# A two-layer diffusion trunk on one core: modulation matmuls of the first stage in 16 blocks, all token transposes ahead of it, small constants loaded later

## The chip, the core and the metric

The kernel runs on one core of a Trainium2 chip. The metric is the device time of one execution in microseconds. Below, PE is TensorE, DVE is VectorE, ACT is ScalarE, POOL is GpSimd and SP is SyncE, which here does nothing but issue DMAs.

## The reference

Two layers work on 256 latent tokens and 256 context tokens of width 2048, all in float32. The change lies in how layer 0 begins:

```python
shift, scale, gate = jnp.split(jax.nn.silu(c) @ w_ada[li] + b_ada[li], 3, axis=-1)
shift_c, scale_c, gate_c = jnp.split(jax.nn.silu(c_ctx) @ w_ada[li] + b_ada[li], 3, axis=-1)
h = rms_norm(x, g_pre[li]) * (1.0 + scale[:, None]) + shift[:, None]
hc = rms_norm(xc, g_pre[li]) * (1.0 + scale_c) + shift_c
p = h @ w_in[li]
pc = hc @ (w_in[li] if need_ctx else w_in[li][:, :N_KV_COLS])
```

After that each layer has four token mixers (windowed attention, latent attention, a recurrence, pooling), a gated merge and an output projection.

## The kernel before

**Products.** Every large product is taken in two halves: a weight tile `raw` is split by `wunit` into `whi` (ACT, L443) and `wlo` (DVE, L445, with L447 for the odd 64 columns), the activations are kept as `hh` and `hl`, and `prod` adds three matmuls of 128x128 by 512 tokens (L458 `whi`·`hh`, L459 `whi`·`hl`, L461 `wlo`·`hh`).

**The first stage.** `chunks_by_k` goes over the 16 blocks of 128 channels two at a time (`k0` = 0, 2, ... 14). For each `k0` it does three groups of four output tiles, positions 0 to 11; eleven tiles have six matmuls, the one at position 7 is 64 wide and has four, so that a step of `k0` has 70 matmuls. Each tile's sum goes to SBUF: by ACT for `k0` = 0 (L496), by a DVE add afterwards (L498). After each tile the generator `pre` is advanced by one piece; it prepares `hh` and `hl` of the next two channel blocks.

**What `pre` does.** `start(k0)` needs scale and shift of 256 channels. `ada_chunk` takes them from the 2048-row product of SiLU(c) and SiLU(c_ctx) with `w_ada`: for scale and for shift four loads of 512 KB (`adaw`, ring of six buffers), each followed by sixteen weight-loads-and-multiplies on 32-column strips (L251; the trace counts eight matmul records to a load). ACT copies the result (`adaS`, L256), PE turns it (`adaT`, L260), DVE reduces it to `aT` and `bT`. Then `prenorm_out` transposes the normalised tokens of these channels on PE (L394, `n000p` and so on), and ACT and DVE make `hh` (L399), a scaled copy (L400) and `hl` (L401) from the PSUM tile. Each of these is a piece of its own behind one output tile: eight visits to `ada` with one load each, two `adaT` pairs, two groups of four transposes per step.

**Order around it.** Tile schedules the instructions; `issued_after(last_main[0])` ties a piece of `pre` to the last matmul ahead of it, `urgent()` raises its priority. SP issues DMAs in order, so a load that waits for its buffer holds those behind it. The small constants (`late_constants`, POOL's queue) are issued once the last token piece is normalised (`after`, L119).

## Time and profile before

| | |
|---|---|
| median of three runs | 2889.99 us (2888.51 to 2897.6) |
| the profiled execution's own time | 2890.45 us |
| its span in the profile | 2888.7 us |
| PE busy | 2817.6 us, 98% of the span |
| DVE / ACT / POOL busy | 1682.4 / 1083.9 / 99.2 us |
| loads and stores | 457.65 MB, mean 158 GB/s |

The span is the profiled execution from its first to its last instruction; 1.75 us of its own time lie around it. In the line of forty slices PE has a 5 in the first slice of 72 us and 9 in nearly all others, while the DMA line begins with 8, 7 and 6, its highest digits.

### The profile page before, as it was taken

The page shows a single profiled execution, that of the slowest core. Times are in us where ns is not written, and L with a number is a line of the kernel's source. Part 1 is how long each engine was busy: PE and PEld are TensorE (multiplying, and loading weights), DVE is VectorE, ACT ScalarE, POOL GpSimd, SP SyncE. Part 2 cuts the span into 40 slices and gives each one's busy share as a digit, 9 for nine tenths or more (in the row PEclk, how much of TensorE's full clock was granted, in tenths as well). Part 3 has the DMA queues.
Part 4 walks back from the last instruction along what each step waited for, and adds up shares of the span by engine and source line. Part 5 has one row for each costly group of instructions (what it writes and reads, how often), then busy time and mean ns, then how long its engine had stood idle before and what let it go on. Part 6 is the DMA issues. An engine that isn't in the chain of part 4 may idle for free.

```text
span 2888.7 us, 40002 instructions
## 1 busy us (share of the span) xinstructions
PE 2817.6 (98%) x15693; PEld 2368.6 (82%) x15693; DVE 1682.4 (58%) x2686; ACT 1083.9 (38%) x1656; POOL 99.2 (3%) x188
## 2 busy tenths in 40 slices
PE   5999999999999999999999999999999999999998
PEld 2567877887787877788888887888789999999997
DVE  2667757777456655565443566667546545554465
ACT  3225644333223222222222345556433444444443
POOL 1000010000000000000000011000200000000000
PEclk9999999999999999999999999999999999999999
DMA  8762215435444544454555457533333666666664
GB/s 275 253 197 81 81 57 168 121 121 161 156 149 138 177 143 153 146 166 156 153 160 159 155 185 244 188 112 87 96 95 114 185 183 190 183 190 184 194 215 166
DMA packets 307276, 457.65 MB, mean 158 GB/s; under 512 B 19976, under 2 KB 131040, under 8 KB 307088
## 3 DMA queue, kind: packets, MB, share of 16 engines
q1 hardware_dynamic: 294848, 429.98, 48.4%
q0 software_dynamic: 7136, 18.64, 2.1%
q10 hardware_dynamic: 5104, 6.48, 0.6%
q8 instruction: 123, 2.02, 0.3%
q14 instruction: 65, 0.53, 0.1%
HBM read 443.40 MB, written 11.62 MB: 158 GB/s over the span
## 4 chain that ended last, share of the span: by engine, by line
PE 82%; issue 6%; DVE 6%; DMA 4%; ACT 1%; POOL 1%; SPq 0%; DVEq 0%; POOLq 0%; ACTq 0%
DMA adv_1w<-in_w_ada_dram 2%; PE L0stps L459 1%; PE ada L251 1%; DVE wlo L445 1%; PE L0stps L458 1%; PE L0stps L461 1%; PE o10p L1138 1%; PE o10p L1139 1%; PE o10p L1137 1%; PE o01p L1138 1%; PE o01p L1139 1%; PE o01p L1137 1%; DMA adv_0w<-in_w_ada_dram 1%; DMA adaw<-in_w_ada_dram 1%; DVE adv_0a L290 1%
## 5 line engine op out<-in xcount | busy, mean ns | idle before, releaser
L443 ACT ACTIVATE whi<-raw 128x1024 fp32r<-128x1024 f32 (+2 forms) x608 | 638.9, 1051 | 1383.5 <-issue 57.7
L445 DVE TENSOR_TENSOR wlo<-raw,whi 128x1024 fp32r<-128x1024 f32 (+1 forms) x608 | 734.2, 1209 | 572.0 <-ACT whi L443 555.3
L290 DVE SCALAR_TENSOR_TENSOR adv_3a<-adv_3w,csil,adv_3a 128x512 f32<-128x512 f32 x105 | 73.8, 747 | 85.9 <-DMA adv_3w<-in_w_ada_dram 85.7
L290 DVE SCALAR_TENSOR_TENSOR adv_1a<-adv_1w,csil,adv_1a 128x512 f32<-128x512 f32 x105 | 74.5, 747 | 78.0 <-DMA adv_1w<-in_w_ada_dram 77.9
L290 DVE SCALAR_TENSOR_TENSOR adv_0a<-adv_0w,csil,adv_0a 128x512 f32<-128x512 f32 x105 | 73.5, 747 | 66.1 <-DMA adv_0w<-in_w_ada_dram 65.8
L290 DVE SCALAR_TENSOR_TENSOR adv_2a<-adv_2w,csil,adv_2a 128x512 f32<-128x512 f32 x105 | 73.8, 747 | 42.9 <-DMA adv_2w<-in_w_ada_dram 42.5
L459 PE MATMUL L0stps<-hl,whi 128*128 128x512 f32 x192 | 79.9, 416 | 3.8 <-DVE hl L401 3.3
L458 PE MATMUL L0stps<-hh,whi 128*128 128x512 f32 x192 | 79.0, 426 | 2.1 <-ACT hh L399 1.0
L461 PE MATMUL L0stps<-hh,wlo 128*128 128x512 f32 x176 | 69.8, 396 | 0.0
L251 PE MATMUL ada<-adaw,csil 128*32 128x256 f32 x512 | 44.2, 425 | 17.6 <-DMA adaw<-in_w_ada_dram 17.6
L458 PEld LDWEIGHTS L0stps<-hh,whi 128*128 128x128 f32 x192 | 36.1, 188 | 25.4 <-issue 14.8
L459 PEld LDWEIGHTS L0stps<-hl,whi 128*128 128x128 f32 x192 | 36.4, 189 | 19.7 <-issue 8.6
L1138 PE MATMUL o01p<-wlo,hh 128*128 128x512 f32 x128 | 50.2, 393 | 2.1 <-DVE wlo L445 2.1
L1138 PE MATMUL o10p<-wlo,hh 128*128 128x512 f32 x128 | 49.9, 390 | 0.5 <-DVE wlo L445 0.5
L1139 PE MATMUL o01p<-whi,hl 128*128 128x512 f32 x128 | 49.9, 390 | 0.0
L1137 PE MATMUL o00p<-whi,hh 128*128 128x512 f32 x128 | 49.9, 390 | 0.0
L1139 PE MATMUL o00p<-whi,hl 128*128 128x512 f32 x128 | 49.9, 390 | 0.0
L1138 PE MATMUL o00p<-wlo,hh 128*128 128x512 f32 x128 | 49.8, 389 | 0.0
L1137 PE MATMUL o10p<-whi,hh 128*128 128x512 f32 x128 | 49.7, 390 | 0.1
L1139 PE MATMUL o10p<-whi,hl 128*128 128x512 f32 x128 | 49.8, 389 | 0.0
L1137 PE MATMUL o01p<-whi,hh 128*128 128x512 f32 x128 | 49.6, 390 | 0.0
L251 PEld LDWEIGHTS ada<-adaw,csil 128*32 128x32 f32 x512 | 11.1, 114 | 43.0 <-issue 27.2
(2355 smaller groups left out, 8434.5 us busy)
## 6 DMA issues: line engine op xcount, KB each, us to landing
raw<-in_w_in_dram SPq DMA_DIRECT2D x352, 512.0 KB, 3.7
raw<-in_w_out_dram SPq DMA_DIRECT2D x96, 512.0 KB, 4.4
adaw<-in_w_ada_dram SPq DMA_DIRECT2D x64, 512.0 KB, 5.3
raw<-in_w_in_dram SPq DMA_DIRECT2D x256, 128.0 KB, 2.4
raw<-in_w_branch_dram SPq DMA_DIRECT2D x64, 512.0 KB, 3.7
adv_0w<-in_w_ada_dram SPq DMA_DIRECT2D x32, 512.0 KB, 3.7
adv_1w<-in_w_ada_dram SPq DMA_DIRECT2D x32, 512.0 KB, 4.2
adv_2w<-in_w_ada_dram SPq DMA_DIRECT2D x32, 512.0 KB, 4.3
```

The source lines that it names most:

```text
L251: last_ada[0] = mm(out=ps[32 * q:32 * q + 32, :256], lhsT=csil32[:, 4 * u + q, :], rhs=raw[:, q, :], start=(u == 0), stop=(u == 3))
L290: stt(out=acc[r], in0=raw[:, kk, :], scalar=sc, in1=acc[r], op0=ALU.mult, op1=ALU.add)
L443: act(out=hi[:, :, :width], in_=raw[:, :, :width], func=AF.Copy)
L445: tt(out=lo[:, :, :w], in0=raw[:, :, :w], in1=hi[:, :, :w].bitcast(F32), op=ALU.subtract)
L458: mm(out=out, lhsT=w, rhs=xh, start=first, stop=False)
L459: last_main[0] = mm(out=out, lhsT=w, rhs=xl, start=False, stop=last and wd == 64)
L461: last_main[0] = mm(out=out, lhsT=lo[:, kk, o:o + 128], rhs=xh, start=False, stop=last)
L1137: mm(out=pss[t], lhsT=a, rhs=hi[:, kk, :], start=(k == 0), stop=False)
L1138: mm(out=pss[t], lhsT=a, rhs=lo[:, kk, :], start=False, stop=False)
L1139: mm(out=pss[t], lhsT=b, rhs=hi[:, kk, :], start=False, stop=(k == KT - 1))
```

## The change

Each modulation product (256 columns of scale or of shift) is issued as one block of its four loads, behind the tiles at positions 0 and 5 of a step; the turn of both, in one PSUM tile with four transposes, stands behind position 7. The transposes of all 16 channel blocks stand ahead of the stage, copied from PSUM to SBUF tiles `n0t` by ACT and DVE in turns; `hh` and `hl` are made from these. For `j` = 0 alone the block is urgent. `late_constants` is called when `hl` of `k0` = 4 has been written.

```diff
--- before.py
+++ after.py
@@ -239,7 +239,7 @@
     def issued_after(ins):
         return tc.issue_after(ins.ins if hasattr(ins, "ins") else ins)
 
-    def ada_chunk(l, part, j, ring):
+    def ada_units(l, part, j, ring):
 
         c0 = part * D + 256 * j
         ps = paux(f"ada{l}_{part}_{j}")
@@ -249,26 +249,28 @@
                 nc.sync.dma_start(out=raw, in_=I["w_ada"][l, 512 * u:512 * u + 512, c0:c0 + 256].rearrange("(k p) n -> p k n", p=128))
             for q in range(4):
                 last_ada[0] = mm(out=ps[32 * q:32 * q + 32, :256], lhsT=csil32[:, 4 * u + q, :], rhs=raw[:, q, :], start=(u == 0), stop=(u == 3))
-            if u < 3:
-                yield
         S_ = slot(f"adaS{l}_{part}_{j}")
-        S = S_[:, :256]
-        act(out=S, in_=ps[:, :256], func=AF.Copy)
-        pt = paux(f"adaT{l}_{part}_{j}")
         with urgent():
+            act(out=S_[:, :256], in_=ps[:, :256], func=AF.Copy)
+        return S_
+
+    def ada_turn(l, j, S1, S0):
+
+        pt = paux(f"adaT{l}_{j}")
+        for i, S_ in enumerate((S1, S0)):
             for q in range(2):
-                nc.tensor.transpose(pt[:, 128 * q:128 * q + 128], S[:, 128 * q:128 * q + 128], ident)
-        free(S_)
-        red = small(f"adar{l}_{part}_{j}").rearrange("p (a b) -> p a b", b=2)
-        nc.vector.tensor_reduce(out=red, in_=pt[:, :256].rearrange("p (c g r) -> p c r g", c=2, g=4)[:, :, 0:2, :], axis=AX.X, op=ALU.add)
-        bias = BT[:, 48 * l + 16 * part + 2 * j:48 * l + 16 * part + 2 * j + 2].unsqueeze(2).to_broadcast([128, 2, 2])
-        if part == 0:
-            tt(out=bT[l][:, 2 * j:2 * j + 2, :], in0=red, in1=bias, op=ALU.add)
-        elif part == 1:
-            tt(out=red, in0=red, in1=bias, op=ALU.add)
-            g = VT[:, 16 * l + 2 * j:16 * l + 2 * j + 2].unsqueeze(2).to_broadcast([128, 2, 2])
-            stt(out=aT[l][:, 2 * j:2 * j + 2, :], in0=red, scalar=1.0, in1=g, op0=ALU.add, op1=ALU.mult)
-        yield
+                nc.tensor.transpose(pt[:, 256 * i + 128 * q:256 * i + 128 * q + 128], S_[:, 128 * q:128 * q + 128], ident)
+            free(S_)
+        for i, part in enumerate((1, 0)):
+            red = small(f"adar{l}_{part}_{j}").rearrange("p (a b) -> p a b", b=2)
+            nc.vector.tensor_reduce(out=red, in_=pt[:, 256 * i:256 * i + 256].rearrange("p (c g r) -> p c r g", c=2, g=4)[:, :, 0:2, :], axis=AX.X, op=ALU.add)
+            bias = BT[:, 48 * l + 16 * part + 2 * j:48 * l + 16 * part + 2 * j + 2].unsqueeze(2).to_broadcast([128, 2, 2])
+            if part == 0:
+                tt(out=bT[l][:, 2 * j:2 * j + 2, :], in0=red, in1=bias, op=ALU.add)
+            else:
+                tt(out=red, in0=red, in1=bias, op=ALU.add)
+                g = VT[:, 16 * l + 2 * j:16 * l + 2 * j + 2].unsqueeze(2).to_broadcast([128, 2, 2])
+                stt(out=aT[l][:, 2 * j:2 * j + 2, :], in0=red, scalar=1.0, in1=g, op0=ALU.add, op1=ALU.mult)
 
     def ada_cols(l, part, j, ring, sums):
 
@@ -483,6 +485,7 @@
             pass
         for k0 in range(0, KT, 2):
             nxt = pre(k0 + 2) if k0 + 2 < KT else iter(())
+            pos = 0
             for gi, (segs, cts, sums) in enumerate(groups):
                 width = max(o + n for o, _, n in segs)
                 hi, lo = wunit([(o, kview(w, k0, c0, n)) for o, c0, n in segs], width)
@@ -496,8 +499,10 @@
                             act(out=sums[i][:, :n], in_=ps, func=AF.Copy)
                         else:
                             tt(out=sums[i][:, :n], in0=ps, in1=sums[i][:, :n], op=ALU.add)
-                    with issued_after(last_main[0]):
-                        next(nxt, None)
+                    if pos in (0, 5, 7):
+                        with issued_after(last_main[0]):
+                            next(nxt, None)
+                    pos += 1
             for _ in nxt:
                 pass
 
@@ -1171,30 +1176,49 @@
 
     for half in range(2):
         prenorm_stats(xs[half], f"n0{half}")
+
+    xt = []
+    for k in range(KT):
+        ps = pmain(f"n0x{k}")
+        for half in range(2):
+            for t in range(2):
+                o = 256 * half + 128 * t
+                nc.tensor.transpose(ps[:, o:o + 128], xs[half][t][k // 4][:, 128 * (k % 4):128 * (k % 4) + 128], ident)
+        xt.append(slot(f"n0t{k}"))
+        if k % 2:
+            act(out=xt[k], in_=ps, func=AF.Copy)
+        else:
+            nc.vector.tensor_copy(out=xt[k], in_=ps)
+        if k % 4 == 3:
+            free(*(xs[half][t][k // 4] for half in range(2) for t in range(2)))
     ada_ring = Ring("d", 6)
 
     def start(k0):
+        j = k0 // 2
+        S_ = []
         for part in (1, 0):
-            steps = ada_chunk(0, part, k0 // 2, ada_ring)
-            while True:
-                with urgent(), issued_after(last_x):
-                    more = next(steps, 0) is None
-                if not more:
-                    break
-                yield
-        for half in range(2):
-            with urgent():
-                prenorm_out(xs[half], 0, half, f"n0{half}{k0}", [k0], 1)
-            if half == 1 and k0 % 8 == 6:
-                if k0 == 14:
-                    free(csil_)
-                    ada_ring.close()
-                for h_ in range(2):
-                    free(*(xs[h_][t][c] for t in range(2) for c in range(k0 // 4 - 1, k0 // 4 + 1)))
+            with urgent() if j == 0 else contextlib.nullcontext(), issued_after(last_x):
+                S_.append(ada_units(0, part, j, ada_ring))
             yield
-
-    with after(xs[1][1][3][:, :1]):
-        late_constants()
+        with urgent():
+            ada_turn(0, j, *S_)
+            for k in (k0, k0 + 1):
+                y = xt[k]
+                for half in range(2):
+                    t0 = 256 * half
+                    a, b = aT[0][:, k, half:half + 1], bT[0][:, k, half:half + 1]
+                    act(out=hh[:, k, t0:t0 + 256], in_=y[:, t0:t0 + 256], func=AF.Identity, scale=a, bias=b)
+                    ts(out=y[:, t0:t0 + 256], in0=y[:, t0:t0 + 256], scalar1=a, scalar2=b, op0=ALU.mult, op1=ALU.add)
+                tt(out=hl[:, k, :], in0=y, in1=hh[:, k, :].bitcast(F32), op=ALU.subtract)
+                free(y)
+        if k0 == 4:
+            with after(hl[:, k0, :1].bitcast(F32)):
+                late_constants()
+        if k0 == 14:
+            free(csil_)
+            ada_ring.close()
+        yield
+
     first = layer(0, start)
     next(first)
     decay_floor()
```

What that does to the order of instructions shows best in three places. First PE in the head. In the names `ada_1_0` is scale and `ada_0_0` shift of the first 256 channels. Before, all of shift stands behind the turn of scale, and one step's transposes follow:

```order
L251 MATMUL ada_1_0_254<-adaw_1_0_3_273,csil_115 32x256 x4
L260 MATMUL adaT_1_0_281<-ident,adaS_1_0_279 128x128 x2
L251 MATMUL ada_0_0_288<-adaw_0_0_0_289,csil_115 32x256 x4
L251 MATMUL ada_0_0_288<-adaw_0_0_1_295,csil_115 32x256 x4
L251 MATMUL ada_0_0_288<-adaw_0_0_2_301,csil_115 32x256 x4
L251 MATMUL ada_0_0_288<-adaw_0_0_3_307,csil_115 32x256 x4
L260 MATMUL adaT_0_0_315<-ident,adaS_0_0_313 128x128 x2
L394 MATMUL n000p_321<-ident,x_80 128x128
L394 MATMUL n010p_332<-ident,x_96 128x128
```

After, both products are through before the first turn, and the transposes of the later channel blocks (`n0x`) stand between them and the stage:

```order
L1186 MATMUL n0x_303<-ident,x_102 128x128
L1186 MATMUL n0x_310<-ident,x_82 128x128
L251 MATMUL ada_1_0_355<-adaw_1_0_3_374,csil_115 32x256 x4
L1186 MATMUL n0x_310<-ident,x_86 128x128
L1186 MATMUL n0x_310<-ident,x_98 128x128
L1186 MATMUL n0x_310<-ident,x_102 128x128
L1186 MATMUL n0x_317<-ident,x_83 128x128
L1186 MATMUL n0x_317<-ident,x_87 128x128
L1186 MATMUL n0x_317<-ident,x_99 128x128
L1186 MATMUL n0x_317<-ident,x_103 128x128
L262 MATMUL adaT_0_409<-ident,adaS_1_0_380 128x128 x2
L1186 MATMUL n0x_324<-ident,x_83 128x128
L1186 MATMUL n0x_324<-ident,x_87 128x128
```

Each load's matmuls now stand between transposes; the first matmul of the stage (`L0stps_0_0`) follows the last of 64 transposes and the second pair of the turn.

Second PE inside a step, here `k0` = 4, where `ada_0_3` is shift for the next one. Before, a visit stands behind each tile:

```order
L458 MATMUL L0stps_1_4_841<-hh,whi_820 128x512
L459 MATMUL L0stps_1_4_841<-hl,whi_820 128x512
L461 MATMUL L0stps_1_4_841<-hh,wlo_821 128x512
L251 MATMUL ada_0_3_834<-adaw_0_3_1_849,csil_115 32x256 x4
L458 MATMUL L0stps_2_4_855<-hh,whi_820 128x512
L459 MATMUL L0stps_2_4_855<-hl,whi_820 128x512
L461 MATMUL L0stps_2_4_855<-hh,wlo_821 128x512
L458 MATMUL L0stps_2_4_855<-hh,whi_820 128x512
L459 MATMUL L0stps_2_4_855<-hl,whi_820 128x512
L461 MATMUL L0stps_2_4_855<-hh,wlo_821 128x512
L251 MATMUL ada_0_3_834<-adaw_0_3_2_863,csil_115 32x256 x4
```

After, one block stands between two tiles, with the tiles of the same group on both sides:

```order
L460 MATMUL L0stps_1_4_900<-hh,whi_886 128x512
L461 MATMUL L0stps_1_4_900<-hl,whi_886 128x512
L463 MATMUL L0stps_1_4_900<-hh,wlo_887 128x512
L251 MATMUL ada_0_3_908<-adaw_0_3_0_909,csil_115 32x256 x4
L251 MATMUL ada_0_3_908<-adaw_0_3_1_915,csil_115 32x256 x4
L251 MATMUL ada_0_3_908<-adaw_0_3_2_921,csil_115 32x256 x4
L251 MATMUL ada_0_3_908<-adaw_0_3_3_927,csil_115 32x256 x4
L460 MATMUL L0stps_2_4_935<-hh,whi_886 128x512
L461 MATMUL L0stps_2_4_935<-hl,whi_886 128x512
L463 MATMUL L0stps_2_4_935<-hh,wlo_887 128x512
L460 MATMUL L0stps_2_4_935<-hh,whi_886 128x512
```

Four visits have become one, and nothing else stands between the tiles until the turn.

Third DVE behind the turn of that step, from the part of the step that gives the shift `bT` on. Before, latent (`n006t`) and context (`n016t`) tokens are scaled from PSUM:

```order
L266 TENSOR_TENSOR bT_159<-adar_0_3_886,BT 128x4
L498 TENSOR_TENSOR L0gd_252<-L0stps_0_4_895,L0gd_252 128x512
L400 TENSOR_SCALAR n006t_908<-n006p_903,aT_157,bT_159 128x256
L498 TENSOR_TENSOR L0gd_252<-L0stps_1_4_914,L0gd_252 128x512
L400 TENSOR_SCALAR n006t_908<-n006p_903,aT_157,bT_159 128x256
L400 TENSOR_SCALAR n016t_927<-n016p_922,aT_157,bT_159 128x256
L401 TENSOR_TENSOR hl<-n006t_908,hh 128x2x256
L498 TENSOR_TENSOR L0gd_253<-L0stps_2_4_933,L0gd_253 128x512
L400 TENSOR_SCALAR n016t_927<-n016p_922,aT_157,bT_159 128x256
L498 TENSOR_TENSOR L0gd_253<-L0stps_3_4_941,L0gd_253 128x512
L401 TENSOR_TENSOR hl<-n016t_927,hh 128x2x256
```

After, scale and shift come from one turn, whose reductions stand right ahead of these rows; a weight split and an add (`L0gd`) stand ahead of `bT`:

```order
L447 TENSOR_TENSOR wlo_1076<-raw_1074,whi_1075 128x2x384
L273 SCALAR_TENSOR_TENSOR aT_157<-adar_1_3_954,VT 128x4
L501 TENSOR_TENSOR L0gd_353<-L0stps_0_4_977,L0gd_353 128x512
L269 TENSOR_TENSOR bT_159<-adar_0_3_958,BT 128x4
L449 TENSOR_TENSOR whi_1075<-raw_1074,whi_1075 128x2x64
L501 TENSOR_TENSOR L0gd_353<-L0stps_1_4_985,L0gd_353 128x512
L1211 TENSOR_SCALAR n0t_280<-n0t_280,aT_157,bT_159 128x256 x2
L1211 TENSOR_SCALAR n0t_287<-n0t_287,aT_157,bT_159 128x256
L1212 TENSOR_TENSOR hl<-n0t_280,hh 128x512
L1211 TENSOR_SCALAR n0t_287<-n0t_287,aT_157,bT_159 128x256
L501 TENSOR_TENSOR L0gd_354<-L0stps_2_4_993,L0gd_354 128x512
L1212 TENSOR_TENSOR hl<-n0t_287,hh 128x512
```

The four scalings now read SBUF tiles `n0t`, one for each channel block, and the second `hl` stands behind the third of the step's `L0gd` adds instead of the fourth.

On SP's queue a step has the same loads: eight `adaw` and three `w_in`. Before, the `adaw` loads come six and two with the `w_in` loads around them; now they come four by four, with one to three `w_in` loads between.

## Rows read from the trace of the kernel before

**Rows 1.** windows of head and first stage, split at steps of `k0`

```profile
0.00:44.51 44.51, 10.84 (x79) 4.05 (x79) 11.27 (x39) 14.70 (x39) 7.75 (x20) 1.00 0.86 274
44.51:71.87 27.36, 25.59 (x146) 15.61 (x147) 8.25 (x18) 12.26 (x21) 0.00 (x0) 0.94 0.85 277
71.87:97.34 25.47, 23.98 (x148) 14.83 (x146) 17.06 (x31) 7.86 (x13) 0.00 (x0) 1.00 0.85 279
...
170.56:194.95 24.39, 24.19 (x147) 14.82 (x146) 15.25 (x28) 5.88 (x9) 0.00 (x0) 1.00 0.75 235
...
219.34:236.55 17.21, 16.55 (x71) 13.06 (x70) 14.76 (x27) 6.25 (x7) 0.00 (x0) 1.00 0.31 80
```

**Rows 2.** waits of TensorE, 0 to 237 us (total us, times, longest us)

```profile
PE ada L251 <- DMA adaw<-in_w_ada_dram: 17.6, 4, 8.0
...
PE L0stps L459 <- DVE hl L401: 3.3, 2, 1.8
```

**Rows 3.** timeline, end of the head (start us, duration us, engine line op, count)

```profile
35.73 1.08 PE L251 MATMUL ada<-adaw,csil 128*32 128x256 f32 x8 [1.88 <-DMA adaw<-in_w_ada_dram]
...
37.99 3.64 PE L251 MATMUL ada<-adaw,csil 128*32 128x256 f32 x32
38.06 1.06 ACT L443 ACTIVATE whi<-raw 128x1024 fp32r<-128x1024 f32 x1 [0.74 <-DMA raw<-in_w_in_dram]
...
42.20 0.44 PE L260 MATMUL adaT<-ident,adaS 128*128 128x128 f32 x2 [0.56 <-ACT adaS L256]
...
44.51 1.20 PE L458 MATMUL L0stps<-hh,whi 128*128 128x512 f32 x4 [1.00 <-ACT hh L399]
```

**Rows 4.** timeline of TensorE, one visit to the modulation product

```profile
53.86 0.39 PE L461 MATMUL L0stps<-hh,wlo 128*128 128x512 f32 x1
54.18 0.64 PE L251 MATMUL ada<-adaw,csil 128*32 128x256 f32 x8
54.75 0.50 PE L459 MATMUL L0stps<-hl,whi 128*128 128x512 f32 x1
55.09 0.39 PE L461 MATMUL L0stps<-hh,wlo 128*128 128x512 f32 x1
```

**Rows 5.** timeline of TensorE, an `adaT` pair and an `n002p` group

```profile
65.92 0.38 PE L260 MATMUL adaT<-ident,adaS 128*128 128x128 f32 x2
66.06 0.47 PE L458 MATMUL L0stps<-hh,whi 128*128 128x512 f32 x1
66.37 0.39 PE L459 MATMUL L0stps<-hl,whi 128*128 128x512 f32 x1
...
66.84 0.60 PE L394 MATMUL n002p<-ident,x 128*128 128x128 f32 x4
67.19 0.48 PE L458 MATMUL L0stps<-hh,whi 128*128 128x512 f32 x1
67.51 0.39 PE L459 MATMUL L0stps<-hl,whi 128*128 128x512 f32 x1
```

**Rows 6.** timeline of TensorE, 47 to 52 us

```profile
49.01 1.08 PE L251 MATMUL ada<-adaw,csil 128*32 128x256 f32 x8
...
50.61 0.63 PE L461 MATMUL L0stps<-hh,wlo 128*128 128x512 f32 x1
```

**Rows 7.** DMA issues, 75 to 219 us (last: median us to landing)

```profile
adaw<-in_w_ada_dram SPq DMA_DIRECT2D x42, 512.0 KB, 4.9
```

**Rows 8.** DMA queues and issues, 0 to 45 us

```profile
q0 software_dynamic: 288, 0.93, 5.6%
...
raw<-in_w_in_dram SPq DMA_DIRECT2D x2, 512.0 KB, 10.0
```

**Rows 9.** VectorE groups by shape, 75 to 219 us (busy us, mean ns)

```profile
L498 DVE TENSOR_TENSOR L0gd<-L0stps,L0gd 128x512 f32<-128x512 f32 x22 | 15.2, 690 | 1.6 <-PE L0stps L461 1.5
...
L400 DVE TENSOR_SCALAR n0012t<-n0012p,aT,bT 128x256 f32<-128x256 f32 x2 | 1.1, 540 | 0.3 <-ACT hh L399 0.3
```

**Rows 10.** timeline of VectorE, four scalings of a 128x512 tile in SBUF

```profile
16.38 1.67 DVE L382 TENSOR_SCALAR x<-x,n00r 128x512 f32<-128x512 f32 x4 [0.73 <-POOL n00r L365]
```

## The prediction

> **What bounds the kernel now.** I read the busy times of the page first: PE is busy in 98% of the span, so a gain is PE time taken away or one of its few gaps closed. The windows, cut at the steps of `k0`, give window, length, then busy time and count of PE, PEld, DVE, ACT and POOL, the granted clock, DMA share and GB/s. The reader is to see in [rows 1] a head of 44.51 us in which PE works 10.84, a first step of 27.36 at a clock of 0.94, a second of 25.47, then steady steps of 24.39 (five lie between 24.37 and 24.46) that are nearly all PE, and a last one of 17.21, in which no modulation is left. In steady steps the DMA engines are at 0.75. The waits of PE over this stretch [rows 2] name loads of `w_ada` (17.6 us in 4 waits, all in the head) and `hl` (3.3 us in 2 waits, at the starts of `k0` = 0 and 2). So there are three places to look at: the head, the two waits on `hl`, and what PE does in a steady step.
>
> **What a steady step consists of.** In the last step 71 matmuls cost 16.55 us of busy PE, .233 each [rows 1]; 70 are 16.3 us. The other 8.1 of 24.39 are work for the next channels, read from start to start. A visit to the modulation product: the tile's last matmul starts at 53.86, the visit at 54.18, the next matmul at 54.75 and its follower at 55.09 [rows 4]. That is .57 for the eight records, and the matmuls ahead of and behind them take .32 and .34 where .23 is normal: .57 + .09 + .11 = .77. An `adaT` pair takes .14, and the matmul behind it .31 instead of .23, so .22; four token transposes take .35 and the next matmul .32, so .44 [rows 5]. Eight visits, two pairs and two groups of four are 6.16 + .44 + .88 = 7.48; with the matmuls 23.8, and .6 remains for small waits.
>
> **Part 1, blocks of 32 records.** [...] I take 2.1, by the row of the same shape. Two blocks for eight visits: 6.16 - 4.2 = 1.96 us a step (1.2 to 2.06). Seven steps have them: 13.7 us.
>
> **Part 2, transposes.** Two groups of four leave each step: .88 x 7 = 6.2 us. The turn's four `adaT` transposes cost about what the two pairs did. In the head 56 more transposes run: at .35 for four 4.9 us, at half clock 9.8, where PE idles 44.51 - 10.84 = 33.7 us [rows 1]; covered if they fit between the loads, otherwise rival C. Their sixteen copies go to ACT and DVE, eight each; by the nearest row, a 128x512 add from PSUM at .69 [rows 9], 5.5 us each, beside 11.27 and 14.70 of 44.51. Covered too.
>
> **Part 3, DVE and ACT in a step.** The scalings now read SBUF. From PSUM one of 256 columns takes .54 [rows 9]; from SBUF one of 512 takes .42 (1.67 for four, [rows 10]). So four cost at most 1.7 us instead of 2.2, but all four, both `hl` and both parts' reductions come behind one turn, with later splits and adds between. Before, half of that was done earlier. PE needs the first `hl` when `k0` turns over, four tiles or some 5.6 us after the turn. A shorter chain with a later start: I put the wait at the boundary as it is now (inside the .6), with bounds of -.5 and +1.0 us a step, -3.5 and +7.
>
> That ACT's `hh` now reads SBUF is not in the trace. [...]
>
> **Part 4, the two waits on `hl`.** The first step is 2.97 longer than a steady one (27.36 - 24.39), of which the longest wait on `hl` is 1.8 [rows 2] and the rest follows from the low clock; the second is 1.08 longer, with the other wait of 1.5. Now `hl` of the first channels comes from ready tiles, and the second turn has its scalings in one run. Bounds: nothing, or all of it (2.97 and 1.08). I take 1.0 of each, the first because the clock stays low after a head that still waits on loads.
>
> **Part 5, the head.** Before, the first four loads of shift stand behind the turn of scale, so PE works 3.64 us on them at 37.99, waits .56 for `adaS`, turns at 42.20 and starts the stage 2.31 later [rows 3]. The `w_in` tile landed just before 38.06, where `whi` begins. Now only the last load's eight remain when it lands: 1.08 + .56 + 2.31, and, for the second half of a common turn, half of the 2.31 again: 5.1 us. If the last load lands no earlier than the `w_in` tile did, the stage starts at 43.2, a gain of 1.3. Besides, .93 MB of constants leave the head on the POOL queue, behind which loads shared the engines: at the head's 274 GB/s 3.4 us [rows 1, 8]. Bounds 1.3 and 4.7; I take 3.5, since most of those bytes were issued beside loads that the stage waits for. The constants move to about 80 us, where DMA has some 20% free and nothing reads them soon: nothing; without that cover 3.4 us.
>
> **Sum.** 13.7 + 6.2 + 1.0 + 1.0 + 3.5 = 25.4 us. The last step has none of this. Behind the stage the order of instructions is the same on every engine, so the gain is passed on. Against the profiled execution's own 2890.45 that is 2865.0; the median of the runs lies .46 below that execution, less than I can tell. A difference under 0.3%, 8.7 us, counts as no change.
>
> **Rivals.**
>
> *B, loads late for the blocks.* A ring of six holds four loads of a block and two of the next; the third of the second block is issued when the first block's first eight have run. From there to its use lie five tiles of 1.40 and the block, 9.6 us; on the other side, from position 5 to the next 0, about 12. For it: `adaw` takes 4.9 us to land in the median [rows 7], but a step of 21.5 us with the same 5.7 MB (24.39 us at 235 GB/s) asks for 265 GB/s, and two `adaw` behind two `w_in` loads, 2.1 MB, take 7.5 us at the 279 that the second step reached. Against it: that step ran so with no wait on `adaw` [rows 1, 2]. If PE waits 1 us at each of 14 blocks: 2879.
>
> *C, head and clock give nothing.* The 64 transposes and a first turn at half clock take up the gain: -3.5 -1.0, and a first step at half clock over some 2 us more, 1.0: 2870.5. For it: after PE had waited, eight records took 1.08 at 49.01 and a matmul .63 at 50.61, twice the normal, though the stage was under way [rows 6]. Against it: transposes between the loads give PE more to do. [...]
>
> *D, the turn's chain late.* Scale, shift, four scalings and two `hl` behind position 7, and `hl` 2.5 us late at seven boundaries: 17.5 us, 2882.5, no change that can be told. For it: the two waits of [rows 2] are on just this. Against it: by [rows 9, 10] the scalings are 1.7, two adds 1.4 and the two `hl` and the reductions, at .42 to .69 an operation, some 3: about 6 us in 5.6 us of tiles and a first matmul. Tight, not 2.5 over.
>
> *E, slower.* SP issues in order. If an `adaw` load waits for its buffer until the first block has run, the `w_in` loads behind it wait too, then their splits, and PE waits for `whi` and not for the block. From 3.6 us a step (25.4 / 7) it is no gain; if a `w_in` tile takes the 10.0 us of the head [rows 8] instead of the 4.9 of a load in the stage, 5.1 us a step, 2901. Against it: in the steps of before the `adaw` loads stood in the same queue and PE had no wait on `whi`.
>
> **How the numbers follow.** Forecast .62, with a range of its own from 2857 (all of parts 4 and 5 and 3.5 at the boundaries: 2.05 + 1.2 + 3.5 = 6.8 lower, and .7 for blocks of 2.05) to 2872 (a block of 2.48 costs 5.3, and 2 at boundaries). B .18, C .10, D .05, E .05. The range holds the forecast and C and reaches to B, 2857 to 2879; outside are D, E, part of B and the forecast's edges, some 2 in 10. Faster: the forecast, C and nearly all of B, .89. Same: D and the rest of B, .06. Slower: E, .05.
>
> **What would show it.** Steps of about 21.5 us instead of 24.39 with two blocks of 32 records, each costing 2.1; no `n00` transposes inside the stage; the first `L0stps` matmul near 41 instead of 44.51; constants landing near 80 us with nothing waiting for them. The prediction is wrong if PE's waits inside the stage name `adaw` (B), `hl` or `hh` beyond .5 a step (D) or `whi` (E), if the low clock reaches into the second step (C), or if a block costs 2.5 or more.

## The result, and the profile after

The changed kernel takes 2863.3 us in the median of four runs (2861.3 to 2865.07), the kernel before beside it 2891.87: a ratio of 0.990, 95% interval 0.9883 to 0.9916, or 28.6 us less. The forecast was 2865.0, 25.4 us below the profiled execution's 2890.45; the profiled execution of the changed kernel took 2861.3, 29.2 less.

Two traces of each kernel (the second ones are the runs `e9_before_again` and `e8_again` below), cut where the first stage begins and ends:

| trace | stage begins at | its length | the part behind it | span |
|---|---|---|---|---|
| before, first | 44.51 | 192.04 | 2652.13 | 2888.7 |
| before, second | 41.21 | 190.93 | 2659.38 | 2891.5 |
| changed, first | 41.46 | 162.57 | 2655.48 | 2859.5 |
| changed, second | 40.93 | 164.31 | 2659.39 | 2864.6 |

Times are microseconds; a stage is cut at its first matmul and at the first instruction of PE behind it. The gain is in the stage, 29.5 us by the first pair of traces and 26.6 by the second. The head and the part behind the stage differ as much between two executions of one kernel (3.3 and 7.3 us for the kernel before) as between the kernels.

The windows of the changed kernel, columns as in [rows 1], cut at the steps of `k0`; they answer to that group:

```profile
0.00:41.46 41.46, 18.64 (x135) 10.29 (x135) 16.31 (x47) 18.96 (x48) 2.98 (x11) 1.00 0.84 269
41.46:63.81 22.35, 22.35 (x139) 16.34 (x139) 9.56 (x20) 13.55 (x23) 0.00 (x0) 0.92 0.95 314
63.81:84.35 20.54, 20.54 (x140) 15.25 (x138) 13.23 (x26) 6.62 (x11) 1.18 (x3) 1.00 0.90 292
84.35:105.60 21.25, 20.72 (x139) 15.14 (x138) 14.56 (x29) 5.82 (x9) 3.67 (x7) 1.00 1.07 362
105.60:126.21 20.61, 20.61 (x140) 15.17 (x138) 14.26 (x29) 5.93 (x9) 0.00 (x0) 1.00 0.95 313
...
188.00:204.03 16.03, 16.03 (x71) 13.06 (x70) 14.30 (x27) 6.89 (x10) 0.00 (x0) 1.00 0.43 109
```

PE is busy in every microsecond of the steps but the third (84.35 to 105.6), where .53 are missing. A steady step takes 20.6 us and not 24.39, the first 22.34 and not 27.36, the last 16.04 and not 17.21. DMA is at .90 to 1.07 in the first four steps, where it was at .85 and then .75 to .77: the same loads come in shorter steps, and the third has the constants besides.

The waits of PE from 17 us to the end of the stage, answering to [rows 2]:

```profile
PE n0x L1186 <- DVE x L384: 4.1, 2, 2.0
PE L0stps L460 <- ACT hh L1210: 2.2, 1, 2.2
PE ada L251 <- DMA adaw<-in_w_ada_dram: 1.5, 3, 0.6
```

The 17.6 us on loads of `w_ada` are 1.5 (1.0 of them in the head), the 3.3 on `hl` are gone; the wait on `hh` at the start of the stage is 2.2 where it was 1.0, and 4.1 on DVE are new: it still normalises the tokens (L384) when PE could turn them.

A block and a turn inside a steady step, PE's timeline, answering to [rows 4, 5]:

```profile
136.31 0.39 PE L463 MATMUL L0stps<-hh,wlo 128*128 128x512 f32 x1
136.63 1.93 PE L251 MATMUL ada<-adaw,csil 128*32 128x256 f32 x32
138.49 0.50 PE L460 MATMUL L0stps<-hh,whi 128*128 128x512 f32 x1
138.83 0.40 PE L461 MATMUL L0stps<-hl,whi 128*128 128x512 f32 x1
...
140.89 0.60 PE L262 MATMUL adaT<-ident,adaS 128*128 128x128 f32 x4
141.25 0.47 PE L460 MATMUL L0stps<-hh,whi 128*128 128x512 f32 x1
141.56 0.39 PE L461 MATMUL L0stps<-hl,whi 128*128 128x512 f32 x1
```

The block lasts 1.86 us from start to start, the matmul behind it .34 instead of .23, the one ahead of it .32: 2.07 with its margins. The turn's four transposes take .36 and .08 behind them.

### The profile page after: what moved, and what is told of

It is laid out like the page before. It is cut to its first block, busy times and chain, and to the rows that moved or that the text cites. A ratio compares the mean times of both kernels' runs of the same rounds, so it can differ in the third digit from the quotient of the medians.

```text
span 2859.5 us, 40013 instructions
## 1 busy us (share of the span) xinstructions
PE 2800.8 (98%) x15693; PEld 2378.8 (83%) x15693; DVE 1679.8 (59%) x2694; ACT 1088.4 (38%) x1664; POOL 99.3 (3%) x188
## 4 chain that ended last, share of the span: by engine, by line
PE 81%; issue 6%; DVE 6%; DMA 6%; ACT 1%; POOL 1%; SPq 0%; DVEq 0%; POOLq 0%; ACTq 0%
DMA adv_3w<-in_w_ada_dram 2%; DMA adv_1w<-in_w_ada_dram 2%; PE L0stps L460 2%; PE L0stps L461 1%; DVE wlo L447 1%; PE L0stps L463 1%; PE ada L251 1%; PE o10p L1143 1%; PE o10p L1144 1%; PE o10p L1142 1%; PE o01p L1143 1%; PE o01p L1144 1%; PE o01p L1142 1%; DVE adv_1a L292 1%; DMA adaw<-in_w_ada_dram 1%
## 5 line engine op out<-in xcount | busy, mean ns | idle before, releaser
L463 PEld LDWEIGHTS L0stps<-hh,wlo 128*128 128x128 f32 x176 | 33.5, 190 | 8.5 <-issue 1.6
L251 PE MATMUL ada<-adaw,csil 128*32 128x256 f32 x512 | 34.2, 398 | 1.5 <-DMA adaw<-in_w_ada_dram 1.5
```

Source lines behind the costliest of these rows:

```text
L251: last_ada[0] = mm(out=ps[32 * q:32 * q + 32, :256], lhsT=csil32[:, 4 * u + q, :], rhs=raw[:, q, :], start=(u == 0), stop=(u == 3))
L463: last_main[0] = mm(out=out, lhsT=lo[:, kk, o:o + 128], rhs=xh, start=False, stop=last)
```

## The experiments

Each edit is against the changed kernel unless the text says otherwise, and each number stands beside the first trace of the changed kernel. The code shows the main lines of an edit; `...` marks what is left out. The runs come in three groups, and the kernel before, measured with each, took 2891.84, 2890.95 and 2892.56 us in the median. Each run has one trace, so a head or a part behind the stage in it can differ by some us without a cause in the edit.

**Visits instead of blocks.** Each product in three visits, six a step instead of two:

```diff
                 last_ada[0] = mm(out=ps[32 * q:32 * q + 32, :256], lhsT=csil32[:, 4 * u + q, :], rhs=raw[:, q, :], start=(u == 0), stop=(u == 3))
+            if u in (1, 2):
+                yield
...
-                    if pos in (0, 5, 7):
+                    if pos in (0, 1, 2, 3, 4, 5, 7):
```

> The changed kernel with each modulation product issued as three visits (two loads, one load, one load) behind positions 0 to 2 and 3 to 5 instead of one block of four; the turn stays behind position 7, the transposes stay in the head. Theory A (a visit costs its margins and a slower first group, so that 32 records in one piece save .34 us for each visit that is left out, .77 - .43): four visits more a step cost 1.4 us, steps of 22.0 instead of 20.60, the total 9.5 us above the changed kernel. Theory B (the visits cost nothing, the step became shorter because the wait on hl at its start is gone): steps stay at 20.6 within .2 and the total within 2 us.

Steps of 22.05 to 22.10 instead of 20.60 (the first, at clock 1.00, 22.36), the last step as before (16.06); the stage is 8.3 us longer, the median 2873.02. Four more visits cost 1.49 us, .37 each. The .34 of theory A takes .43 for eight more records in a block, which is what the changed kernel's trace has: (1.86 - .57) / 3, with .57 for eight alone (96.72 to 97.29). Theory A holds, B falls. The total came out 9.7 us above the changed kernel's, as A said.

**Transposes in the steps.** The two channel blocks of a step are turned behind its `adaT` and read from PSUM; the loop that turned all of them in the head is gone:

```diff
             for k in (k0, k0 + 1):
-                y = xt[k]
+                ps = paux(f"n0x{k}")
+                for half in range(2):
+                    for t in range(2):
+                        o = 256 * half + 128 * t
+                        nc.tensor.transpose(ps[:, o:o + 128], xs[half][t][k // 4][:, 128 * (k % 4):128 * (k % 4) + 128], ident)
+                y = slot(f"n0t{k}")
...
-                    act(out=hh[:, k, t0:t0 + 256], in_=y[:, t0:t0 + 256], func=AF.Identity, scale=a, bias=b)
-                    ts(out=y[:, t0:t0 + 256], in0=y[:, t0:t0 + 256], scalar1=a, scalar2=b, op0=ALU.mult, op1=ALU.add)
+                    act(out=hh[:, k, t0:t0 + 256], in_=ps[:, t0:t0 + 256], func=AF.Identity, scale=a, bias=b)
+                    ts(out=y[:, t0:t0 + 256], in0=ps[:, t0:t0 + 256], scalar1=a, scalar2=b, op0=ALU.mult, op1=ALU.add)
```

> The changed kernel with the transposes of two channel blocks back in each step, behind the adaT transposes of the turn, and hh and the scalings reading PSUM; the blocks of 32 and the one turn stay. The prediction's term: the eight transposes cost .88 to .92 us a step, steps of 21.5, with no wait on hl at the start of a step. Theory A (the wait on hl at the start of a step, .75 us in the kernel before, went away because the scalings read ready tiles in SBUF): .9 + .75, steps of 22.2, and the last step back from 16.04 to about 17.2. Theory B (it went away because scale and shift come in one turn): steps of 21.5 and the last step at 16.1. The head: 41.5 if the transposes there are covered, 40.5 or less if they hold the stage up.

Its windows (head and a steady step):

```profile
0.00:37.27 37.27, 12.00 (x79) 4.31 (x79) 11.37 (x40) 15.22 (x41) 2.97 (x11) 1.00 0.90 286
...
145.98:167.68 21.70, 21.70 (x148) 15.96 (x146) 15.04 (x28) 5.88 (x9) 0.00 (x0) 1.00 0.80 262
```

A steady step takes 21.70, 1.10 more, the last 16.25, .2 more. The end of the head, the turn with the transposes behind it in a steady step, and the start of the last step:

```profile
31.72 1.08 PE L251 MATMUL ada<-adaw,csil 128*32 128x256 f32 x8 [0.36 <-DMA adaw<-in_w_ada_dram]
...
139.19 0.60 PE L262 MATMUL adaT<-ident,adaS 128*128 128x128 f32 x4
139.63 1.04 PE L1196 MATMUL n0x<-ident,x 128*128 128x128 f32 x8
140.42 0.48 PE L460 MATMUL L0stps<-hh,whi 128*128 128x512 f32 x1
...
189.42 0.39 PE L460 MATMUL L0stps<-hh,whi 128*128 128x512 f32 x1
189.89 0.50 PE L461 MATMUL L0stps<-hl,whi 128*128 128x512 f32 x1
```

From the turn to the next tile there are 1.23 us, where the turn alone took .36: the eight transposes cost .87, as priced. The other .2 is not theirs. It lies in gaps between the tiles' matmuls, and the last step, which has no transposes, has it too: its first matmul with `hl` starts .47 after the step's first instead of .22. Most of the wait at a step's start stays away, so theory A falls and the steps are near those of B; reading from PSUM brings back .2 at most. But the stage begins at 37.27: 56 transposes that the head no longer has were not covered there. The stage ends at 205.68, 1.65 us later than in the changed kernel: it begins 4.2 earlier and is 5.8 longer. The median is 2867.31.

**Constants early.** `late_constants` in the head, as before:

```diff
-        if k0 == 4:
-            with after(hl[:, k0, :1].bitcast(F32)):
-                late_constants()
...
+    with after(xs[1][1][3][:, :1]):
+        late_constants()
     xt = []
```

> The changed kernel with the small constants loaded in the head again, as before. The prediction's term: 2.2 of its 3.5 us for the head are the constants (3.4 at most), so the first stage begins at 43.7 instead of 41.46 (44.9 at most). Rival (the loads of the head are covered by the transposes, and the stage waits for ACT, which copies shift at 38.38 though its product was through at 35.62): 41.5 to 42.0. In both the third step loses its .53 us wait on a load and falls from 21.25 to 20.6.

The window of its third step:

```profile
83.90:104.40 20.50, 20.50 (x139) 15.25 (x138) 14.54 (x29) 5.81 (x9) 0.00 (x0) 1.00 0.98 332
```

The stage begins at 41.00, not later, and the third step takes 20.51 (20.50 between these cuts) instead of 21.25. The median is 2861.25. The rival holds by this trace: the constants cost nothing in this head. The first `w_in` tile took 7.5 us to land instead of 5.8, but it landed at 34.56, and its split `whi` stands behind other work on ACT until 35.97. Where the change put the constants the DMA engines have nothing free (1.07): in the changed kernel the loads of the third step make PE wait .53 us in the first trace, and that step takes 21.81 in the second.

**Four buffers for `adaw`.**

```diff
-    ada_ring = Ring("d", 6)
+    ada_ring = Ring("d", 4)
```

> The changed kernel with four instead of six buffers for the loads of w_ada, so that no load of the next block is in flight before the block ahead of it has begun. Theory A (rival B of the prediction is near: loads take 8 to 9 us to land in the stage now, and the first of a block is issued 9 us before its use): PE waits for adaw at most blocks, 1 to 3 us each, 14 to 40 us in all. Theory B (loads come in time with room to spare): no waits in the stage, the total as the changed kernel within 2 us apart from the head, which has two loads less in flight.

Steps of 20.77 to 23.17, PE waits 3.5 us for `adaw` in five waits inside the stage, the longest 1.2; the stage is 5.1 us longer (167.65) and begins at 43.32, the median 2871.16. Neither theory's sizes fit: the loads do come late, but by .25 us a block in the mean. With six buffers rival B stayed at .53 us in the first trace and .9 in the second.

**`hl` by halves of the tokens.** The order of the kernel before inside a step, in the changed one:

```diff
-            for k in (k0, k0 + 1):
-                y = xt[k]
-                for half in range(2):
+            for half in range(2):
+                for k in (k0, k0 + 1):
...
-                tt(out=hl[:, k, :], in0=y, in1=hh[:, k, :].bitcast(F32), op=ALU.subtract)
+                for k in (k0, k0 + 1):
+                    tt(out=hl[:, k, t0:t0 + 256], in0=xt[k][:, t0:t0 + 256], in1=hh[:, k, t0:t0 + 256].bitcast(F32), op=ALU.subtract)
```

> The changed kernel with hh, the scalings and hl of a step made by halves of the tokens (latent tokens of both channel blocks first, context tokens after), as the kernel before did, instead of by channel blocks; one more subtraction of 256 columns for each 512. Theory A (the wait of PE on hl at the start of a step went away because the first matmuls need one channel block alone, whose hl is now done first): hl of the first block is complete only some 1.0 to 1.5 us after the first matmul, steps of 20.9 to 21.35 instead of 20.60 and PE waits on hl by name or in spacings; the total 2 to 5 us longer. Theory B (the wait went away because both reductions come from one turn): steps of 20.6 to 20.7, the total within 1 us.

Steady steps of 21.05 to 21.13, the last 16.53, both .5 more; the median is 2865.35, which the spread does not tell from the changed kernel, so that the total of theory A is not shown. The start of a step, on PE:

```profile
149.73 0.97 PE L460 MATMUL L0stps<-hh,whi 128*128 128x512 f32 x3
150.85 0.50 PE L461 MATMUL L0stps<-hl,whi 128*128 128x512 f32 x1 [0.15 <-DVE hl L1213]
```

From the first matmul to the first with `hl` there are 1.12 us for three matmuls that need .68; the wait is back, partly under the name `hl` and partly as the slower matmul behind it. By the steps theory A holds.

**Late transposes.** The last four, or eight, channel blocks behind the first turn (`tokens` is the body of the loop over `k`; shown for four):

```diff
-    for k in range(KT):
+    for k in range(12):
+        tokens(k)
...
                 free(y)
+        if k0 == 0:
+            for k in range(12, KT):
+                with issued_after(last_turn[0]):
+                    tokens(k)
```

> The changed kernel with the transposes of the last four channel blocks issued behind the first turn instead of ahead of it. Theory A (in the head the transposes, their copies on ACT and the turn stand in each other's way: shift was copied 2.8 us after its product, and PE then idles 2.2 us ahead of the stage, which leaves the clock low for its first 3 us): the 16 transposes fill that gap, 1.75 us, the stage begins at 38.5 to 40 instead of 41.46 and the first step falls from 22.34 to 20.6 to 21.2; the total 3 us below the changed kernel. Rival (the stage waits for the loads and the chain of the turn, wherever the transposes stand): 41.0 to 41.5, the first step as now or 1 us shorter.

> As the run with four late channel blocks, with eight of them behind the first turn: 32 transposes, 3.5 us, where PE idled 2.2. Theory A: the head ahead of the turn is as short as with the transposes in the steps (the stage began at 37.27 there, with 1.56 us of idle PE ahead of it), plus 3.5 - 1.56: the stage begins at 39.2, the first step takes 20.6 to 21.2, the total 3 to 4 us below the changed kernel. Rival: 41.0 to 41.5 as above.

With four the stage begins at 37.74, earlier than expected, and its first step, which then waits 1.0 us for the head's last copies, takes 22.24, longer than expected; with eight it begins at 39.66 and the first step takes 20.64, as its window shows:

```profile
39.66:60.30 20.64, 20.64 (x141) 15.34 (x140) 8.61 (x18) 12.52 (x22) 0.00 (x0) 1.00 1.07 357
```

PE is busy throughout and the granted clock is 1.00, where the changed kernel shows .92. The stages end at 200.56 and 200.26, 3.5 and 3.8 us earlier than in the changed kernel. The median with four, 2859.6, is 3.7 us below the changed kernel's, as expected; that with eight, 2864.97, is 1.7 above it. In the traces the part behind the stage was 2659.2 and 2661.1, 3.7 and 5.6 us longer than in the changed kernel's first, so it can hide such a gain; what it was in the other executions is not known.

**The same kernels again.**

> The changed kernel once more, for a second trace of it. Theory A (what is lost behind the stage is lost in the merges of layer 0, by the chance of an execution, where DVE stands on a load of w_ada while PE waits for it): stage and steps alike within .3 us, the part behind the stage different from that of the first trace by 1 us or more. Theory B (it is a fixed price of arriving earlier): the part behind the stage 2655.5 within .5 us.

> The kernel before once more, for a second trace of it. Theory A (what lies behind the first stage varies from execution to execution by some us in the merges of layer 0, and the first trace of before was at the short end of it): steps as in the first trace, the part behind the stage longer than its 2652.1 by 1 to 5 us. Theory B (the changed kernel pays something fixed behind the stage): 2652.1 within .5 us, so that the changed kernel's 2655.5 and 2659.4 are 3 to 7 us of its own.

The times are in the table above; the medians were 2865.53 and 2894.21. Not all was alike within .3 us: the first step of the changed kernel took 23.48 (clock .87) and the third 21.81. Behind the stage both second traces give 2659.4. Theory A holds in both, in the kernel before by more than it said (7.3 us and not 1 to 5): the difference of 3.35 us between the first traces can't be called a price of the change.

**Without the later modulation products.** Seven of eight loads of `adv` and their DVE accumulations are left out, in the kernel before and in the changed one:

```diff
         for u in range(8):
+            if u:
+                if u < 7:
+                    yield
+                continue
             raw = wp.tile([128, 2, 512], F32, name=f"{nm}w{u}", tag="raw", bufs=4)
```

> The kernel before with seven of eight loads and accumulations of the later modulation products (adv, DVE) left out, so that later modulations are partial sums. If those loads make DVE and then PE wait in the merges of layer 0: PE's waits there on L1078 and L1049 (4.9 us in three of .8 to 2.2 between the first merge and the last, with half the clock behind them) shrink to under 1 us, and the part behind the stage is 5 us or more shorter than 2652.1. If the waits have another cause: they stay.

> The changed kernel with the same loads and accumulations left out. Theory A (its loss behind the stage comes from those loads): the part behind the stage is within .5 us of that of the kernel before without them. Theory B (another, fixed price): 3 us or more longer.

The part behind the stage is 2636.6, 15.5 us shorter than in the first trace of before, and 2634.9, and in the merges of layer 0 PE has no gap of over .1 us in either, where it had 4.9 to 11.5 us of them with `adv`. What else shrank there was not taken apart. The two are 1.7 us apart, more than theory A's .5, but with the changed kernel ahead; without these loads a price of 3 us is excluded. The first of these loads is issued behind the first stage, so heads and stages are those of the unedited kernels, a third pair: the stage is 192.09 and 163.82 long and begins at 42.42 and 44.32, later in the changed kernel.

**Both helpful edits together.** Eight late channel blocks and early constants:

> The changed kernel with both things that helped: eight channel blocks' transposes behind the first turn, and the small constants loaded in the head. If both add up: the stage begins at 39.2 to 39.7, the first step takes 20.6, the third 20.5 to 20.6, the stage ends at 199.7 instead of 204.03 and 205.24, 4.3 to 5.5 us earlier; the median 2858 to 2861, within what the part behind the stage varies. If the constants are in the way of the loads now that the head is shorter: the stage begins at 41 or later.

The stage begins at 41.07, its first step takes 21.61, the third 20.64, and it ends at 202.31. The median is 2861.55, the ratio to the kernel before 0.9889 (0.9874 to 0.9905), which overlaps that of the changed kernel. The sum of the two gains did not come: the stage begins 1.4 us later than with eight late channel blocks alone. Here `whi` waits for its load, .95 us and there .22, and starts at 35.41 instead of 34.11, because the first `w_in` tile landed 1.3 us later. Of these .85 are a later issue (28.06 and 27.21), ahead of the first constant's at 28.25; the other .46, 7.33 us from issue to landing instead of 6.87, are the most that the constants can have cost this tile.

## Why the prediction was right, point by point

**Blocks: right.** 2.07 us against 2.1, and .37 against .34 for each visit left out. The 2.1 of the sum, like the 2.05 and 2.48 of its range, was the author's estimate and stands in no run: the one block of 32 in the trace of before took 3.64 us, in the head [rows 3]. What the runs showed in its place, in the changed kernel's stage, is 1.86 for 32 records and .57 for eight, so .43 for each further eight, and 2.07 for a block with its margins.

**Transposes in the steps: right in size, wrong as to cover.** .88 us were forecast to leave a step and .87 come back when they are put back. The step that failed is "covered if they fit between the loads": of the head's 33.7 us of idle PE 14.0 are two waits ahead of the first token, which PE turns at 17.6 us in the changed kernel. The head of the changed kernel:

```profile
35.05 0.64 PE L251 MATMUL ada<-adaw,csil 128*32 128x256 f32 x8
...
36.96 1.06 ACT L445 ACTIVATE whi<-raw 128x1024 fp32r<-128x1024 f32 x1
...
38.38 0.40 ACT L254 ACTIVATE adaS<-ada 128x256 f32<-128x256 f32 x1
...
40.32 2.08 ACT L1210 ACTIVATE hh<-n0t,bT,aT 128x256 fp32r<-128x256 f32 x4 [1.05 <-DVE aT L273]
...
41.46 1.35 PE L460 MATMUL L0stps<-hh,whi 128*128 128x512 f32 x4 [2.19 <-ACT hh L1210]
...
43.66 0.63 PE L460 MATMUL L0stps<-hh,whi 128*128 128x512 f32 x1
```

The last eight records of shift start at 35.05, and not because of a load: PE is at work without a gap from 29.57 on, mostly on tokens. With the transposes in the steps such records start at 31.72. In the changed kernel they are through at 35.62 (35.05 and .57), but their copy `adaS` runs at 38.38, because a token copy, the split `whi` and another token copy stand ahead of it on ACT; then come the turn, the reductions, `hh`, and the stage at 41.46, with PE idle for the last 2.19 us. So the transposes held the chain twice, on PE and by their copies on ACT, and the forecast counted busy shares alone. This was rival C's first half. With the transposes in the steps the stage began at 37.27, with four channel blocks late at 37.74, both earlier than in any of the traces with all transposes in the head (40.93 to 44.32). A single trace moves by 3.4 us with the loads, so 4 us is the size by one trace each and not an exact price. Counted from the landing of the first `w_in` tile the forecast had 5.1 us to the stage. It took 7.6 and 6.8 in the two traces of the changed kernel (6.5 and 6.1 before), and 4.2 both with the transposes in the steps and with four channel blocks late.

**The clock: rival C's second half was there, but small.** After the 2.19 us wait the matmuls at 43.66 take .63, where those of a steady step take .39; the window of the first step shows .92, in the second trace .87. With eight late channel blocks, which give PE transposes in that place, the same step has 1.00 and takes 20.64 instead of 22.34 and 23.48: a price of 1.7 us in one trace and 2.8 in the other. The head was not slow until its loads ended: eight records take 1.08 us up to 27.35 and .64 from 29.94 on, with transposes between the loads. In the run without these transposes eight still take 1.08 at 31.72. The length of a wait alone does not tell the clock here: the first step shows 1.00 after 1.78 us of idle PE in the run of six visits and .93 after 1.79 with the ring of four, and the kernel before shows .94 and 1.00 in its two traces after the same waits of 1.0 and 1.8.

**The start of a step: the term that was mis-sized.** The wait was to stay "as it is now", inside the .6 of a step that the forecast left for small waits, with a bound of -.5; nearly all of it went. The .6 was too small itself: it comes from .233 us for a matmul, a mean of the last step with the slower matmuls at its start (.49 us at 220.84, .50 at 221.44), where matmuls in a dense stretch start .227 apart. The steps became 3.79 us shorter and not 2.84. PE at the start of `k0` = 10, first in the kernel before:

```profile
170.56 1.45 PE L458 MATMUL L0stps<-hh,whi 128*128 128x512 f32 x4
172.10 0.50 PE L459 MATMUL L0stps<-hl,whi 128*128 128x512 f32 x1
172.44 0.40 PE L461 MATMUL L0stps<-hh,wlo 128*128 128x512 f32 x1
```

then in the changed kernel:

```profile
146.79 0.39 PE L460 MATMUL L0stps<-hh,whi 128*128 128x512 f32 x1
...
147.47 0.62 PE L460 MATMUL L0stps<-hh,whi 128*128 128x512 f32 x2
147.93 0.68 PE L461 MATMUL L0stps<-hl,whi 128*128 128x512 f32 x2
148.44 0.40 PE L463 MATMUL L0stps<-hh,wlo 128*128 128x512 f32 x1
```

Before, four matmuls that need only `hh` are put first, the first with `hl` starts 1.54 us after the step's start instead of .91, and .34 instead of .23 go to the next. Afterwards the first seven matmuls start .23 apart. DVE shows why. Before:

```profile
169.08 0.68 DVE L401 TENSOR_TENSOR hl<-n0010t,hh 128x512 fp32r<-128x512 f32 x1
...
170.76 0.69 DVE L498 TENSOR_TENSOR L0gd<-L0stps,L0gd 128x512 f32<-128x512 f32 x1
171.37 0.68 DVE L401 TENSOR_TENSOR hl<-n0110t,hh 128x512 fp32r<-128x512 f32 x1
```

`hl` is made by halves of the tokens. The second half is subtracted at 171.37, .81 us after the step began, and every matmul with `hl` needs both halves. After:

```profile
145.85 0.68 DVE L1212 TENSOR_TENSOR hl<-n0t,hh 128x512 fp32r<-128x512 f32 x1
...
146.78 0.68 DVE L501 TENSOR_TENSOR L0gd<-L0stps,L0gd 128x512 f32<-128x512 f32 x1
147.38 0.68 DVE L1212 TENSOR_TENSOR hl<-n0t,hh 128x512 fp32r<-128x512 f32 x1
```

`hl` is made by channel blocks. The first is done at 146.53, ahead of the step's start at 146.79, and serves the first tile; the second is done at 148.06, when the seventh matmul wants it (148.16). The run by halves puts .5 us a step back, and the run that reads PSUM .2 at most: the greater part is the cut by channel blocks, which the diff showed and the forecast read over. The margin is .1 us. Summed from start to start, with .227 for each matmul, the extra time at the first tiles of a steady step fell from .78 to .08 us. Of the surplus of .95 us a step (3.79 - 2.84) these are .70, of which the run by halves accounts for .5; why the other .2 went was not tested. Visits and blocks are .11 (6.21 became 4.14, 2.07 less and not 1.96), and .11 is spread over the other tiles' matmuls; the transposes and the turn came out as priced within .03. The last step gained 1.17, where nothing had been forecast, and the run by halves takes .49 of it back.

**SBUF for `hh`.** The sum had no term for it. The traces have .591 us for each of 16 `hh` that read SBUF against .558 to .569 from PSUM before, about 26 ns more (33 against the run that reads PSUM, .558). It cost nothing, since `hh` is done .84 us ahead of the step.

**The two waits on `hl`.** 1.0 each was forecast. Beyond the 3.79 of a steady step the first step gained 1.23 and the second 1.14 by the first pair of traces. By the second pair the second step gained 1.3 beyond it, but the first step 1.4 less: the kernel before had its clock at 1.00 there (25.85) and the changed kernel at .87 (23.48). The second term was right; the first is the clock's, and whether it gives anything on average is not shown.

**The head: mis-sized.** 3.5 us were forecast, of which 2.2 for the constants. The first traces show 3.05, the second .28, the pair without the later modulation products -1.9, and the constants early cost nothing (41.00): no gain of the head is shown. The `w_in` tile did come sooner after its issue (5.8 and 6.2 us instead of 11.7 and 9.8), but `whi` ran 3.1 and 2.3 us after its landing, since ACT was not free. "Nothing" for the constants at 80 us was wrong too: the free 20% of DMA was that of the old, longer steps, and the third step lost .65 us in the first trace and 1.2 in the second.

**Behind the stage: right as far as the runs tell, though the first traces spoke against it.** 3.35 us seemed to be given back. In the merges of layer 0, DVE stands on a load of `w_ada` with the merge's own work queued behind it. In the first trace of the changed kernel, DVE's timeline:

```profile
1163.15 0.69 DVE L1054 TENSOR_TENSOR L0m3y<-L0m3gps,L0m3y 128x512 f32<-128x512 f32 x1
1167.14 0.75 DVE L292 SCALAR_TENSOR_TENSOR adv_1a<-adv_1w,csil,adv_1a 128x512 f32<-128x512 f32 x1 [3.30 <-DMA adv_1w<-in_w_ada_dram]
1167.81 0.68 DVE L1055 TENSOR_TENSOR L0m3y<-L0m3y,L0m3ob 128x512 f32<-128x512 f32 x1
1168.41 0.68 DVE L1054 TENSOR_TENSOR L0m3y<-L0m3gps,L0m3y 128x512 f32<-128x512 f32 x1
```

3.30 us of waiting for `adv_1w` lie between two operations of the merge (L1054, L1055), and PE waits 2.9 us, to 1169.15, for the L1054 that begins at 1168.41. The sums vary with the execution; PE's waits in this stretch, second trace of the changed kernel:

```profile
PE L0m1mg2ps L460 <- DVE L0m1sg L1083: 3.9, 1, 3.9
PE L0m3gps L460 <- DVE L0m1sg L1083: 2.4, 1, 2.4
PE L0m3mg0ps L460 <- DVE L0m3y L1054: 2.3, 1, 2.3
PE L0m3mg2ps L460 <- DVE L0m3sg L1083: 1.7, 1, 1.7
PE L0m1mg3ps L460 <- DVE L0m1sg L1083: 1.2, 1, 1.2
```

and second trace of the kernel before:

```profile
PE L0m1mg2ps L458 <- DVE L0m1sg L1078: 3.0, 1, 3.0
PE L0m3mg2ps L458 <- DVE L0m3sg L1078: 3.0, 1, 3.0
PE L0m3gps L458 <- DVE L0m1sg L1078: 1.8, 1, 1.8
PE L0m3mg0ps L458 <- DVE L0m3y L1049: 1.2, 2, 0.8
```

11.5 us in one and 9.2 in the other, against 8.4 and 4.9 in the first traces: 3.1 us of the 3.9 by which the two traces of the changed kernel differ behind the stage, and 4.3 of the 7.3 for the kernel before.

**The sum.** In the stage 21.9 us were forecast and 26.6 to 29.5 measured, in the head 3.5 and -1.9 to 3.05: the stage's surplus, mostly the wait at the start of steps, pays for what the head did not give. That the total was right within 1.7 us is in part luck, two errors of opposite sign; the gain by the medians, 28.6, is 3.2 above the forecast 25.4. Rival B came to .53 and .9 us, D and E to nothing: PE never waited for `whi`.

## What to carry to other kernels

When a producer's output is cut into pieces, look at which cut the first consumer needs: `hl` by channel block let the next step begin with half the work done, and that was worth .5 us a step, more than half of what the transposes cost there (.88). Idle time of an engine covers moved work only where its inputs are already there (14.0 of the 33.7 us here lay ahead of the first token) and where neither the work nor its followers stand ahead of the critical chain (here copies on ACT, ahead of an `adaS` that ran 2.76 us after its product). Before a few microseconds far from the edit are explained, trace the unchanged kernel twice.

## What the runs showed that was not expected

Two traces of the kernel before differ by 3.3 us in the head and 7.3 us behind the first stage, with spans only 2.8 us apart; shares of a gain below some 4 us can't be read from one trace of each. The DMA engines moved 292 to 362 GB/s in the first four steps of the changed kernel, where 233 to 279 were enough before; loads then landed after 9.4 us in the median in the third step, against 4.9 in [rows 7], and still came in time but for .53 us.
